# Memory of the RWKV chain becomes ten slots for experts' matrices during the attention, and their loads are issued between its blocks

## Chip, core and metric

The kernel runs on one core of one Trainium2 chip. The metric is the device time of one execution in microseconds (us); lower is better.

## What is computed

One layer of a hybrid encoder on 512 tokens of width 1024, all in float32:

```python
h = rmsnorm(x, norm1_g)
p = h @ w_in                                  # 5504 columns
p_rwkv, q, k, v, gate_logits = split(p)
y_a = rwkv7_bidirectional(p_rwkv, ...) @ w_o_rwkv
y_b = neighbourhood_attention_2d(q, k, v, ...) @ w_o_na
g_a, g_b = split(sigmoid(gate_logits + b_gate))
x = x + (g_a * y_a + g_b * y_b) @ w_out
x = x + hierarchical_moe(rmsnorm(x, norm2_g), ...)   # 32 experts: gate, up, down
```

The last part routes each token to two of 32 experts. An expert is silu(h @ w_gate) * (h @ w_up), times w_down.

## The kernel before

**Stages.** norm1 makes hT, the normalized and transposed input, as a high and a low part. The projection by w_in goes in 43 tiles of 128 columns (proj, L301). Each needs a load of its raw weights on SyncE's queue (w_raw, wraw, 512 KB, two buffers), a high part on ScalarE (ACT, w_hi, L185), a low part (w_lo, L188) on VectorE (DVE), or on GpSimd (POOL) from tile 15 on, and 24 matmuls of 128x512 on TensorE (PE). Tiles 0 to 14 feed the RWKV recurrence; 15 to 42 are the `others` (L759): q, k and v of the attention, then the gates. A gate's result is evacuated from its PSUM bank by ACT (oth) and spilled to DRAM (d_oth). The last nine tiles, 34 to 42, are called b to j here. Matmuls of the `others` have low priority and fill the gaps of the chain and of the attention. The recurrence's second half, `chain(1)`, ends in chain_out, which stores ya (d_ya). The attention (na_attention, L825) goes over two groups of heads and four blocks of columns each, and stores yb (d_yb).

**After the attention.** out_gated (L916) loads ya and yb again (ya_f, yb_f), splits them in high and low parts, multiplies by w_o_rwkv and w_o_na (in_wo) and by the gates (ga, gb), which are fetched from d_oth. out_rows (L977) multiplies by w_out, adds x, transposes and starts the router. Then moe (L1319) works through 16 pairs of experts, 64 rows each: six matrices of 1 MB for a pair (two with gate and up, one down, for each of two experts), 96 in all. It gathers rows xe, transposes them, computes G (gate and up), sg and Yd (down), and adds the result to the output by a scatter. tasks (L1159), called in the second pair, computes a table on VectorE and stores it with SyncE (tab, tabi).

**Slots.** The 96 matrices go through NSLOT = 21 slots (tiles ws0 to ws20) in the order of USE; matrix i takes the slot of matrix i - 21. load_upto(n) (L1242) issues loads until n are out. The slots come in three pools: NS1 = 8 opened after the attention, NS2 = 6 after out_gated, the other 7 after the route. out_gated issues five loads, spread over its eight steps; out_rows issues up to 14 in all; moe issues the rest, after each pair up to 6(p + 1) + 4 + NSLOT.

**What sets the order.** A scheduler orders each engine's instructions by priority and by the order in which the code emits them. Each engine's queue is then fixed: an instruction that waits holds up all behind it. SyncE (SP) issues all loads and stores but the gathers and scatters. Memory is laid out by pools on a left and a right side, and a tile that lies where another has lain waits for that one's last use. The chain's pools are ch (T, 64 KB of each partition; R, 32 KB; O) and cw. Tiles rp (constants, oth) lie left of them.

Of the kernel before, what the change touches and what calls it, by code (L numbers as in the profile page):

```python
# [28 lines left out]
WARM = 12  # L29
NX = 3  # L30
NY = 2
NSLOT = 21
NS1, NS2 = 8, 6
NL1, NL2 = 5, 7
LAG = 2
NT2 = 6
EM05 = float(np.exp(-0.5))
# [141 lines left out]
class K:  # L179
# [645 lines left out]
    def na_attention(self):  # L825
        self.yb = [self.dram.tile([P, 2, 4, P], F32, name="d_yb%d" % i) for i in range(2)]
        for h4 in range(2):
            self.na_inputs(h4)
            for b in range(4):
                self.na_block(h4, b)  # L830
                if 4 * h4 + b < OTH[3]:
                    self.others(1)
        self.others(28, ("x", "mm"))

    def na_block(self, h4, b):
# [80 lines left out]
    def out_gated(self, opz, opw):  # L916

        nc = self.nc
        yaT, ybT = [[opz.tile([P, 4, T], F32R, name="y%s_%s" % (c, n)) for n in ("hi", "lo")] for c in "ab"]

        def part_a(yt):
            t = self.fetch(self.ya[yt], opz.tile([P, T], F32, name="ya_f", tag="ga", bufs=3))
            self.split([y[:, yt] for y in yaT], t)

        def part_b(h4, b, n):
            t = opz.tile([P, 2, n, P], F32, name="yb_f", tag="ga", bufs=3)
            nc.sync.dma_start(t, self.yb[h4][:, :, b:b + n])
            self.split([y[:, 2 * h4:2 * h4 + 2, b * P:(b + n) * P].rearrange("p a (n c) -> p a n c", n=n) for y in ybT], t)

        part_a(0)  # L930
        part_a(1)
        part_b(0, 0, 2)
        part_b(0, 2, 2)
        part_a(2)
        part_a(3)
        part_b(1, 0, 2)
        part_b(1, 2, 1)
        part_b(1, 3, 1)
        self.zT = zT = [[opw.tile([P, 4, T], F32R, name="z%d%s" % (i, n)) for n in ("hi", "lo")] for i in range(2)]
        nat = lambda a: a.rearrange("p (b r c) -> p r b c", b=4, r=8)  # L940
        acc = []

        def open_m(m):
            w = self.wload(m, "wo")
            acc.append((w, [self.bank("mm", [P, T], 4) for c in range(2)]))

        def add(m, c, ks):
            (hi, lo), ps = acc[m]
            y = (yaT, ybT)[c]
            for k in ks:  # L950
                l = [t[:, 4 * c + k] for t in (hi, lo)]
                self.mm3(ps[c], l, [nat(t[:, k]) if c else t[:, k] for t in y], k == 0, k == 3)


        for m in range(2):
            open_m(m)
            for c in range(2):
                add(m, c, range(2))
        for m in range(8):
            if m >= 2:  # L960
                open_m(m)
            for c in (1, 0):
                add(m, c, range(2 if m < 2 else 0, 4))
            pa, pb = acc[m][1]
            ga = self.fetch(self.gate[m], opz.tile([P, T], F32, name="ga", tag="ga", bufs=3))
            gb = self.fetch(self.gate[8 + m], opz.tile([P, T], F32, name="gb", tag="ga", bufs=3))
            self.stt(ga, ga, 1.0, pa, OP.add, OP.mult)
            self.stt(gb, gb, 1.0, pb, OP.add, OP.mult)
            self.tt(ga, ga, gb, OP.add)
            z = [t[:, m % 4] for t in zT[m // 4]]  # L970
            self.act(z[0], ga, AF.Copy, scale=0.5)
            self.stt(z[1], ga, 0.5, z[0].bitcast(F32), OP.mult, OP.subtract)
            if m == 1:
                self.route_setup()
            self.load_upto(NL1 * (m + 1) // 8)

    def out_rows(self):  # L977

        nc, op, zT = self.nc, self.op, self.zT
        x1 = []  # L980
        for tt in range(4):
            x1.append(op.tile([P, D], F32, name="x1_%d" % tt))
            nc.sync.dma_start(x1[-1], self.A["x"][tt * P:(tt + 1) * P])
        rl = self.bank("lg", [P, 4, 36], 1)
        ss = op.tile([P, 2, 4], F32, name="r_ss")

        def post(n, tt, ps):

            x = x1[tt][:, n * T:(n + 1) * T]
            self.tt(x, ps, x, OP.add)  # L990
            sl = slice(tt * P, (tt + 1) * P), slice(n * T, (n + 1) * T)
            nc.sync.dma_start(self.A["out"][sl], x)
            self.act(ps, x, AF.Square, scale=1.0 / 32, accum_out=ss[:, n, tt:tt + 1])
            if n + tt == 0:

                self.act(op.tile([P, 1], F32, name="r_tab"), ss[:, 0, 0:1], AF.Sqrt)
            pt = self.bank("mm", [P, 4, P], 4) if n == 1 and tt >= 2 else self.bank("tp", [P, 4, P], 2)
            for k in range(4):
                self.tr(pt[:, k], x[:, k * P:(k + 1) * P])
            xT = op.tile([P, 4, P], F32, name="x1T", tag="x1T", bufs=2)  # L1000
            if n == 1 and tt == 3:
                nc.vector.tensor_copy(xT[:, 0:2], pt[:, 0:2])
                self.act(xT[:, 2:4], pt[:, 2:4])
            elif tt % 2 == 1:
                self.act(xT, pt)
            else:
                nc.vector.tensor_copy(xT, pt)
            for k in range(4):
                self.mm(rl[:, tt], xT[:, k], self.wr[:, 4 * n + k], start=(n + tt + k == 0), stop=(n == 1 and tt + k == 6),
                        skip_group_check=True)  # L1010
            xg = op.tile([P, T], F32, name="r_xg", tag="r_xg", bufs=2)
            self.tt(xg, x, self.g2[:, sl[1]], eng=nc.gpsimd)
            nc.sync.dma_start(self.h2[sl], xg)

        for n in range(2):
            ps = [self.bank("mm", [P, T], 4) for tt in range(4)]
            w = {}
            for m2 in range(4):
                with self.low(-LOW):
                    hi, lo = [w_.rearrange("p (a k) b -> p a (k b)", a=2) for w_ in self.wload(4 * n + m2, "w_out")]  # L1020
                for i in range(2):
                    w[2 * m2 + i] = hi[:, i], lo[:, i]

                ms = [2 * m2, 2 * m2 + 1] if n == 0 or m2 < 2 else range(4, 8) if m2 == 3 else []
                steps = [(m, tt) for m in ms for tt in range(4)]
                for m, tt in sorted(steps, key=lambda u: u[::-1]) if len(ms) == 4 else steps:
                    sl = slice(tt * P, (tt + 1) * P)
                    self.mm3(ps[tt], tuple(t[:, m % 4, sl] for t in zT[m // 4]), w[m], m == 0, m == 7)
                    if m == 7 and tt >= LAG:
                        post(n, tt - LAG, ps[tt - LAG])  # L1030
                self.load_upto(min(NS1 + NS2, NL1 + (NS1 + NS2 - NL1) * (4 * n + m2 + 1) // NL2))
            for tt in range(4 - LAG, 4):
                post(n, tt, ps[tt])
        st = self.st
        self.stt(st, ss[:, 0], 1e-6, ss[:, 1], OP.add, OP.add)
        self.act(st, st, AF.Sqrt)
        nc.vector.reciprocal(st, st)
        lg = op.tile([P, 4, 36], F32, name="r_lg")
        self.tt(lg, rl, st[:, :, None].to_broadcast([P, 4, 36]))
        self.tt(lg, lg, self.br[:, None].to_broadcast([P, 4, 36]), OP.add)  # L1040
        self.route(lg)
# [324 lines left out]
def build(tc, A):  # L1366
    with ExitStack() as ctx:
        k = K(tc, A, ctx)
# [5 lines left out]
        with ExitStack() as c2:  # L1374
            k.hpool = c2.enter_context(tc.tile_pool(name="hp", bufs=1, side="right"))
            with tc.tile_pool(name="n1", bufs=1) as n1:
                k.norm1(n1)
            k.rp = c2.enter_context(tc.tile_pool(name="rp", bufs=1))
            k.ch = c2.enter_context(tc.tile_pool(name="ch", bufs=1))
            k.cw = c2.enter_context(tc.tile_pool(name="cw", bufs=1))  # L1380
            with tc.tile_pool(name="tmp", bufs=1, side="right") as k.tmp:
                k.rwkv()
            with tc.tile_pool(name="na", bufs=1, side="right", reuse_waits="tile") as k.na:
                k.na_setup()
                k.chain(1)
                k.chain_out(1)
                k.na_attention()
        k.psum_next()
        k.rt = ctx.enter_context(tc.tile_pool(name="rt", bufs=1, reuse_waits="tile"))
        k.wslot, k.slot, k.loaded = [], [], 0  # L1390
        k.slots_open(ctx.enter_context(tc.tile_pool(name="w1", bufs=1, reuse_waits="tile")), NS1)
        cr, cwo = ExitStack(), ExitStack()
        opw = cwo.enter_context(tc.tile_pool(name="opw", bufs=1, side="right", reuse_waits="tile"))
        k.op = cr.enter_context(tc.tile_pool(name="op", bufs=1, side="right", reuse_waits="tile"))
# [35 lines left out]
```

## Time and profile before

| | us |
|---|---|
| median of 3 runs | 939.39 |
| lowest, highest run | 938.81, 946.36 |
| profiled execution | 942.74 |
| its span | 940.6 |

PE is busy 87% of the span, VectorE 46%, ACT 33%, POOL 19%. The profile reads so: a row of a timeline is start, length, engine, line, operation, output<-inputs, count, and in brackets the idle time before it and what ended it. PE is TensorE, PEld its weight loads, SPq the issues of SyncE. In a table of windows a row is the window, its length, the busy time (and instructions) of PE, PEld, DVE, ACT and POOL, the granted clock of TensorE as a share of 2.4 GHz, the mean busy share of the DMA engines, and GB/s. Lines are those of the kernel before; up to the removed lines, the same code stands one line higher after the change.

### The profile page before, as it was taken

The page shows a single profiled execution, that of the slowest core. Times are in us where ns is not written, and L with a number is a line of the kernel's source. Part 1 is how long each engine was busy: PE and PEld are TensorE (multiplying, and loading weights), DVE is VectorE, ACT ScalarE, POOL GpSimd, SP SyncE. Part 2 cuts the span into 40 slices and gives each one's busy share as a digit, 9 for nine tenths or more (in the row PEclk, how much of TensorE's full clock was granted, in tenths as well). Part 3 has the DMA queues.
Part 4 walks back from the last instruction along what each step waited for, and adds up shares of the span by engine and source line. Part 5 has one row for each costly group of instructions (what it writes and reads, how often), then busy time and mean ns, then how long its engine had stood idle before and what let it go on. Part 6 is the DMA issues. An engine that isn't in the chain of part 4 may idle for free. (4 is left out here: it accounts for less than half of the span.)

```text
span 940.6 us, 17281 instructions
## 1 busy us (share of the span) xinstructions
PE 817.8 (87%) x7192; PEld 526.8 (56%) x7192; DVE 430.7 (46%) x870; ACT 309.0 (33%) x667; POOL 177.6 (19%) x154
## 2 busy tenths in 40 slices
PE   8999887889988987799998999999489999788884
PEld 7676655556666655566676678878333333233321
DVE  5698883565689588224446405732412111011000
ACT  6444521223433553035747623232211121011101
POOL 2611121120003132132312330012302112111001
PEclk9999995999998999699999999999689999999998
DMA  6321121121122322322314648889877999999982
GB/s 223 101 64 40 35 101 36 57 69 57 36 68 71 121 68 67 118 80 63 103 51 129 205 138 311 306 314 368 339 314 273 389 395 401 395 403 401 403 337 42
DMA packets 49774, 176.17 MB, mean 187 GB/s; under 512 B 7584, under 2 KB 14368, under 8 KB 37664
## 3 DMA queue, kind: packets, MB, share of 16 engines
q1 hardware_dynamic: 45088, 166.66, 48.1%
q0 software_dynamic: 4608, 8.40, 3.7%
q8 instruction: 57, 0.93, 0.4%
q14 instruction: 21, 0.17, 0.1%
HBM read 159.30 MB, written 24.12 MB: 195 GB/s over the span
## 5 line engine op out<-in xcount | busy, mean ns | idle before, releaser
L200 PE MATMUL G<-ws,xT 128*64 128x512 f32 x512 | 131.4, 603 | 11.0 <-DMA ws<-in_wgu 9.3
L200 PE MATMUL mm<-hT_hi,w_lo 128*128 128x512 f32 x264 | 114.2, 433 | 7.9 <-ACT oth L185 6.8
L188 POOL TENSOR_TENSOR w_lo<-w_raw,w_hi 128x1024 fp32r<-128x1024 f32 x29 | 70.6, 2435 | 241.6 <-ACT w_hi L185 241.6
L200 PE MATMUL mm<-hT_hi,w_hi 128*128 128x512 f32 x264 | 111.9, 424 | 0.0
L200 PE MATMUL mm<-hT_lo,w_hi 128*128 128x512 f32 x264 | 111.8, 423 | 0.0
L200 PEld LDWEIGHTS G<-ws,xT 128*64 128x64 f32 x512 | 42.4, 138 | 87.3 <-issue 64.6
L200 PE MATMUL Yd<-ws,hT 128*64 128x512 f32 x256 | 68.2, 606 | 8.2 <-ACT y L185 8.2
L185 ACT ACTIVATE w_hi<-w_raw 128x1024 fp32r<-128x1024 f32 x59 | 62.3, 1055 | 29.5 <-PE mm L200 29.0
L200 PEld LDWEIGHTS mm<-hT_hi,w_lo 128*128 128x128 f32 x264 | 52.1, 197 | 26.3 <-issue 15.4
L188 DVE TENSOR_TENSOR w_lo<-w_raw,w_hi 128x1024 fp32r<-128x1024 f32 x30 | 37.1, 1237 | 50.7 <-ACT w_hi L185 50.7
L200 PEld LDWEIGHTS mm<-hT_lo,w_hi 128*128 128x128 f32 x264 | 52.0, 197 | 12.8 <-issue 2.2
L200 PEld LDWEIGHTS mm<-hT_hi,w_hi 128*128 128x128 f32 x264 | 52.0, 197 | 11.5 <-issue 1.7
L188 DVE TENSOR_TENSOR sg<-sg,G 128x256 f32<-128x256 f32 x16 | 6.7, 420 | 109.4 <-ACT sg L185 109.4
L1362 POOL DMA_INDIRECT out<-y,idx x16 | 25.3, 1580 | 135.5 <-DVE y L195 106.9
L185 ACT ACTIVATE sg<-G,wts 128x256 f32<-128x256 f32 x16 | 7.6, 473 | 117.7 <-PE G L200 117.7
L648 DVE COPY R<-c 32x128 f32<-32x128 f32 x64 | 18.7, 293 | 54.0 <-ACT R L185 53.3
L200 PE MATMUL c<-R,T 128*32 128x64 f32 (+1 forms) x992 | 36.3, 231 | 7.9 <-DVE nrs_i L191 2.2
L195 DVE TENSOR_SCALAR y<-Yd,wts 128x512 f32<-128x512 f32 (+1 forms) x16 | 11.8, 734 | 68.2 <-PE Yd L200 61.6
L200 PEld LDWEIGHTS Yd<-ws,hT 128*64 128x64 f32 x256 | 17.4, 136 | 44.4 <-ACT y L185 21.2
L200 PE MATMUL tp<-T,KB 64*64 64x128 f32 x512 | 35.0, 281 | 7.3 <-ACT T L185 7.1
L200 PEld LDWEIGHTS c<-R,T 128*32 128x32 f32 (+1 forms) x992 | 26.2, 125 | 26.5 <-issue 14.0
L185 ACT ACTIVATE T<-tp 64x256 f32<-64x256 f32 x64 | 23.9, 377 | 45.0 <-DVE T L188 44.1
(312 smaller groups left out, 1465.5 us busy)
## 6 DMA issues: line engine op xcount, KB each, us to landing
ws<-in_wgu SPq DMA_DIRECT2D x64, 1024.0 KB, 19.6
ws<-in_wd SPq DMA_DIRECT2D x30, 1024.0 KB, 21.0
w_raw<-in_w_in SPq DMA_DIRECT2D x43, 512.0 KB, 3.7
d_oth<-oth SPq DMA_DIRECT2D x16, 256.0 KB
w_raw<-in_wo SPq DMA_DIRECT2D x8, 512.0 KB, 3.8
w_raw<-in_w_out SPq DMA_DIRECT2D x8, 512.0 KB, 5.7
x_in<-in_x SPq DMA_DIRECT2D x4, 512.0 KB, 6.8
ga<-d_oth SPq DMA_DIRECT2D x8, 256.0 KB
```

The source lines that it names most:

```text
L185: self.nc.scalar.activation(out, in_, func, **kw)
L188: (eng or self.nc.vector).tensor_tensor(out, a, b, op=op)
L195: self.nc.vector.tensor_scalar(out, a, s1, None, op0=op0)
L200: return self.nc.tensor.matmul(out, l, r, start=start, stop=stop, **kw)
L648: self.nc.vector.tensor_copy(R[u, :, blk, p2], ps[u, 2:4])
L1362: self.nc.gpsimd.indirect_dma_start(out=self.A["out"], out_offset=bass.IndirectOffsetOnAxis(ap=idx, axis=0), in_=y, in_offset=None, bounds ...
```

## The change

The pools ch and cw get a context of their own (c3) and are closed after the chain's last use, before na_attention. In their place lie the pool rt and the ten slots of w1 (NS1 = 10 instead of 8). na_attention issues the loads of these ten, one or two after each block. out_gated issues none. out_rows issues one a step, to 15 in all (NS2 = 5); the third pool still has 7 slots, so NSLOT is 22. The pool rp moves to the right side, and na is opened in c2. The tiles of out_gated (opz) lie higher by 16 KB of each partition, over the attention's nam, bias, qT and kT instead of the chain's T and R. VectorE's eight small operations of rwkv_consts, which need rp, no longer wait for norm1's memory, and move ahead of the scales of norm1's tiles 1 to 3. On POOL, the copies into T move ahead of the second projection's w_lo.

```diff
--- before.py
+++ after.py
@@ -29,9 +29,8 @@
 WARM = 12
 NX = 3
 NY = 2
-NSLOT = 21
-NS1, NS2 = 8, 6
-NL1, NL2 = 5, 7
+NSLOT = 22
+NS1, NS2 = 10, 5
 LAG = 2
 NT2 = 6
 EM05 = float(np.exp(-0.5))
@@ -830,6 +829,7 @@
                 self.na_block(h4, b)
                 if 4 * h4 + b < OTH[3]:
                     self.others(1)
+                self.load_upto(NS1 * (4 * h4 + b + 1) // 8)
         self.others(28, ("x", "mm"))
 
     def na_block(self, h4, b):
@@ -972,7 +972,6 @@
             self.stt(z[1], ga, 0.5, z[0].bitcast(F32), OP.mult, OP.subtract)
             if m == 1:
                 self.route_setup()
-            self.load_upto(NL1 * (m + 1) // 8)
 
     def out_rows(self):
 
@@ -1028,7 +1027,7 @@
                     self.mm3(ps[tt], tuple(t[:, m % 4, sl] for t in zT[m // 4]), w[m], m == 0, m == 7)
                     if m == 7 and tt >= LAG:
                         post(n, tt - LAG, ps[tt - LAG])
-                self.load_upto(min(NS1 + NS2, NL1 + (NS1 + NS2 - NL1) * (4 * n + m2 + 1) // NL2))
+                self.load_upto(NS1 + min(NS2, 4 * n + m2 + 1))
             for tt in range(4 - LAG, 4):
                 post(n, tt, ps[tt])
         st = self.st
@@ -1375,20 +1374,21 @@
             k.hpool = c2.enter_context(tc.tile_pool(name="hp", bufs=1, side="right"))
             with tc.tile_pool(name="n1", bufs=1) as n1:
                 k.norm1(n1)
-            k.rp = c2.enter_context(tc.tile_pool(name="rp", bufs=1))
-            k.ch = c2.enter_context(tc.tile_pool(name="ch", bufs=1))
-            k.cw = c2.enter_context(tc.tile_pool(name="cw", bufs=1))
-            with tc.tile_pool(name="tmp", bufs=1, side="right") as k.tmp:
-                k.rwkv()
-            with tc.tile_pool(name="na", bufs=1, side="right", reuse_waits="tile") as k.na:
+            k.rp = c2.enter_context(tc.tile_pool(name="rp", bufs=1, side="right"))
+            with ExitStack() as c3:
+                k.ch = c3.enter_context(tc.tile_pool(name="ch", bufs=1))
+                k.cw = c3.enter_context(tc.tile_pool(name="cw", bufs=1))
+                with tc.tile_pool(name="tmp", bufs=1, side="right") as k.tmp:
+                    k.rwkv()
+                k.na = c2.enter_context(tc.tile_pool(name="na", bufs=1, side="right", reuse_waits="tile"))
                 k.na_setup()
                 k.chain(1)
                 k.chain_out(1)
-                k.na_attention()
+            k.rt = ctx.enter_context(tc.tile_pool(name="rt", bufs=1, reuse_waits="tile"))
+            k.wslot, k.slot, k.loaded = [], [], 0
+            k.slots_open(ctx.enter_context(tc.tile_pool(name="w1", bufs=1, reuse_waits="tile")), NS1)
+            k.na_attention()
         k.psum_next()
-        k.rt = ctx.enter_context(tc.tile_pool(name="rt", bufs=1, reuse_waits="tile"))
-        k.wslot, k.slot, k.loaded = [], [], 0
-        k.slots_open(ctx.enter_context(tc.tile_pool(name="w1", bufs=1, reuse_waits="tile")), NS1)
         cr, cwo = ExitStack(), ExitStack()
         opw = cwo.enter_context(tc.tile_pool(name="opw", bufs=1, side="right", reuse_waits="tile"))
         k.op = cr.enter_context(tc.tile_pool(name="op", bufs=1, side="right", reuse_waits="tile"))
```

ACT, before, from the evacuation of projection d to that of h. Here oth_5215, 5325, 5425, 5516 and 5618 are the evacuations of d, e, f, g and h; w_hi_5396, 5487, 5589 and 5624 the splits of the weights of f, g, h and i.

```order
L185 ACTIVATE oth_5215<-mm_5190,hb_229 128x512
L185 ACTIVATE w_hi_5396<-w_raw_5394 128x1024
L185 ACTIVATE yb_5531<-tp_5580 64x256
L185 ACTIVATE ya_hi_5724<-ya_f_5748 128x512
L185 ACTIVATE yb_hi_5726<-yb_f_5752 128x2x256
L185 ACTIVATE yb_hi_5726<-yb_f_5756 128x2x128
L185 ACTIVATE oth_5325<-mm_5300,hb_229 128x512
L185 ACTIVATE w_hi_5487<-w_raw_5485 128x1024
L185 ACTIVATE yb_hi_5726<-yb_f_5760 128x2x128
L185 ACTIVATE oth_5425<-mm_5400,hb_229 128x512
L185 ACTIVATE w_hi_5589<-w_raw_5587 128x1024
L185 ACTIVATE oth_5516<-mm_5491,hb_229 128x512
L185 ACTIVATE w_hi_5624<-w_raw_5622 128x1024
L185 ACTIVATE oth_5618<-mm_5593,hb_229 128x512
```

After, from the evacuation of e on. Here oth_5348, 5449, 5541 and 5644 are e, f, g and h; w_hi_5420, 5512, 5615, 5652 and 5687 the splits of f, g, h, i and j.

```order
L184 ACTIVATE oth_5348<-mm_5323,hb_229 128x512
L184 ACTIVATE w_hi_5420<-w_raw_5418 128x1024
L184 ACTIVATE w_hi_5512<-w_raw_5510 128x1024
L184 ACTIVATE oth_5449<-mm_5424,hb_229 128x512
L184 ACTIVATE w_hi_5615<-w_raw_5613 128x1024
L184 ACTIVATE oth_5541<-mm_5516,hb_229 128x512
L184 ACTIVATE oth_5644<-mm_5619,hb_229 128x512
L184 ACTIVATE w_hi_5652<-w_raw_5650 128x1024
L184 ACTIVATE w_hi_5687<-w_raw_5685 128x1024
```

The split of f has moved from behind the evacuation of d to behind that of e, that of i from behind g to behind h; the splits of ya and yb are no longer between them.

SP, before, around the load of f's weights (w_raw_5394) to that of g's (w_raw_5485).

```order
L288 DMA w_raw_5394<-in_w_in 128x1024
L904 DMA d_yb1_4815<-yb_5340 256x1x128
L560 DMA bvr_4798<-d_bv2_3178 128x512
L560 DMA gr_4801<-d_g2_1076 128x512
L560 DMA bvr_4806<-d_bv3_4012 128x512
L560 DMA gr_4809<-d_g3_1082 128x512
L556 DMA d_oth20_5115<-oth_5113 128x512
L556 DMA d_ya2_4804<-y_4768 128x512
L288 DMA w_raw_5485<-in_w_in 128x1024
```

SP, after, from the slot ws4 on, with f's weights (w_raw_5418); oth_5236 and oth_5348 are d and e.

```order
L1260 DMA ws4_4826<-in_wd 128x2048
L555 DMA d_ya2_4804<-y_4768 128x512
L555 DMA d_ya3_4812<-y_4769 128x512
L904 DMA d_yb1_4833<-yb_5261 256x1x128
L555 DMA d_oth21_5238<-oth_5236 128x512
L1260 DMA ws5_4827<-in_wd 128x2048
L904 DMA d_yb1_4833<-yb_5364 256x1x128
L287 DMA w_raw_5418<-in_w_in 128x1024
L1260 DMA ws6_4828<-in_wgu 128x2048
```

The load of f's weights stood ahead of a store of yb and of the fetches for the chain's output; now it stands behind the evacuation of d and behind the load of ws5.

SP in moe, before, around the store of the table. Loads into ws0 to ws6 here are second uses of these slots, so 26 loads are issued ahead of it (21 first uses, and 0 to 3 and 6).

```order
L1261 DMA ws20_6650<-in_wgu 128x2048
L1261 DMA ws0_5707<-in_wgu 128x2048
L1261 DMA ws1_5708<-in_wd 128x2048
L1261 DMA ws2_5709<-in_wd 128x2048
L1261 DMA ws3_5710<-in_wgu 128x2048
L1261 DMA ws6_5713<-in_wgu 128x2048
L1186 DMA tab_6777<-t_tab_6767 128x2
L1187 DMA tabi_6778<-t_ti_6774 128x2
L1261 DMA ws4_5711<-in_wgu 128x2048
```

The same place after, where slots 0 to 3, 6 and 7 are used again ahead of the table, 28 loads in all.

```order
L1260 DMA ws0_4822<-in_wd 128x2048
L1260 DMA ws1_4823<-in_wd 128x2048
L1260 DMA ws2_4824<-in_wgu 128x2048
L1260 DMA ws3_4825<-in_wgu 128x2048
L1260 DMA ws6_4828<-in_wd 128x2048
L1260 DMA ws7_4829<-in_wd 128x2048
L1185 DMA tab_6779<-t_tab_6769 128x2
L1186 DMA tabi_6780<-t_ti_6776 128x2
L1260 DMA ws4_4826<-in_wgu 128x2048
L1260 DMA ws5_4827<-in_wgu 128x2048
```

Two more loads stand ahead of the table's store than before: one more first use and one more second use.

## Rows read from the trace of the kernel before

**Rows 1.** Windows of 20 us (columns as said under the profile above)
```profile
540.00:560.00 20.00, 18.51 (x80) 15.05 (x81) 0.00 (x0) 6.18 (x8) 7.18 (x3) 1.00 0.43 138
720.00:740.00 20.00, 20.00 (x89) 6.89 (x86) 3.07 (x5) 2.83 (x5) 5.08 (x4) 1.00 1.02 402
840.00:860.00 20.00, 15.89 (x62) 5.09 (x59) 2.08 (x4) 2.61 (x5) 2.63 (x2) 1.00 1.01 397
```

**Rows 2.** PE's timeline in the experts
```profile
740.81 0.51 PE L1300 MATMUL tp<-cst,sg 128*128 128x128 f32 x2
...
753.93 0.50 PE L1300 MATMUL tp<-cst,sg 128*128 128x128 f32 x2
...
860.26 0.50 PE L1300 MATMUL tp<-cst,sg 128*128 128x128 f32 x2 [1.02 <-DVE sg L188]
...
871.70 3.65 PE L200 MATMUL G<-ws,xT 128*64 128x512 f32 x14 [0.81 <-DMA ws<-in_wgu]
876.37 0.51 PE L1300 MATMUL tp<-cst,sg 128*128 128x128 f32 x2 [1.02 <-DVE sg L188]
```

**Rows 3.** The page's DMA issues: KB each, median us to landing
```profile
ws<-in_wgu SPq DMA_DIRECT2D x64, 1024.0 KB, 19.6
...
w_raw<-in_w_in SPq DMA_DIRECT2D x43, 512.0 KB, 3.7
...
w_raw<-in_w_out SPq DMA_DIRECT2D x8, 512.0 KB, 5.7
```

**Rows 4.** SP's timeline around the table's store, route to experts
```profile
667.51 24.65 SPq L1261 DMA_DIRECT2D ws<-in_wgu  x4
...
708.82 0.34 SPq L1186 DMA_DIRECT2D tab<-t_tab  x1
```

**Rows 5.** A window of 4 us behind the table's store
```profile
708.00:712.00 4.00, 3.23 (x18) 1.03 (x16) 1.43 (x9) 0.69 (x1) 0.00 (x0) 1.00 0.23 53
```

**Rows 6.** Timeline of ACT, POOL and PE around projections e to i
```profile
533.12 0.69 ACT L185 ACTIVATE oth<-mm,hb 128x512 f32<-128x512 f32 x1 [2.32 <-PE mm L200]
533.70 1.05 ACT L185 ACTIVATE w_hi<-w_raw 128x1024 fp32r<-128x1024 f32 x1
...
553.03 0.69 ACT L185 ACTIVATE oth<-mm,hb 128x512 f32<-128x512 f32 x1 [5.01 <-issue]
...
534.83 2.39 POOL L188 TENSOR_TENSOR w_lo<-w_raw,w_hi 128x1024 fp32r<-128x1024 f32 x1 [4.33 <-ACT w_hi L185]
...
533.95 0.47 PE L200 MATMUL mm<-hT_hi,w_lo 128*128 128x512 f32 x1 [0.87 <-ACT oth L185]
...
552.78 0.39 PE L200 MATMUL x<-hT_hi,w_lo 128*128 128x512 f32 x1
```

**Rows 7.** PE's timeline at two long waits, and the windows behind them
```profile
105.27 1.36 PE L200 MATMUL tp<-T,KB 64*64 64x128 f32 x16 [2.76 <-ACT T L185]
...
301.37 1.12 PE L203 MATMUL c<-cst,yc 128*128 128x128 f32 x4 [4.08 <-POOL yc L188]
...
105.90:109.30 3.40, 3.40 (x29) 2.37 (x23) 2.72 (x6) 1.14 (x3) 0.00 (x0) 0.51 0.02 5
301.30:307.30 6.00, 5.93 (x18) 4.98 (x19) 4.08 (x6) 3.88 (x15) 2.79 (x2) 0.50 0.34 108
```

**Rows 8.** POOL's and PE's timeline at the start
```profile
14.82 0.95 POOL L354 MEMSET O<- 128x1024 f32 x1 [14.36 <-PE Y L200]
...
18.94 2.40 POOL L188 TENSOR_TENSOR w_lo<-w_raw,w_hi 128x1024 fp32r<-128x1024 f32 x1 [2.81 <-ACT w_hi L185]
21.41 3.81 POOL L360 COPY T<-id 64x2048 f32<-64x2048 f32 x2
...
21.39 0.50 PE L200 MATMUL mm<-hT_hi,w_lo 128*128 128x512 f32 x1 [0.29 <-POOL w_lo L188]
...
28.54 0.50 PE L200 MATMUL x<-hT_hi,w_lo 128*128 128x512 f32 x1 [1.41 <-DVE w_lo L188]
```

**Rows 9.** PE's timeline, out_gated's and out_rows' border
```profile
613.69 0.50 PE L200 MATMUL mm<-w_lo,z0hi 128*128 128x512 f32 x1 [1.13 <-DVE gb L191]
```

## Prediction

> **What bounds the kernel now.** I read the windows of 20 us first. In the last projections TensorE (PE) is busy 18.51 of 20 us at full clock, and the DMA engines carry 0.43 of what they can [rows 1]. In the experts' first half (720 to 740) PE is busy for all 20 us, and the DMA engines too (1.02); at 840 to 860 PE has only 15.89 us of work, with the DMA at 1.01 and 397 GB/s. So three stages have three limits: projections go by PE, the first pairs of experts by PE, the last pairs by the loads. PE's timeline says the same: a pair of experts takes 13.12 us where nothing waits (740.81 to 753.93) and 16.11 us later (860.26 to 876.37), with a wait that a load of ws ends [rows 2]. A matrix is 1,024 KB [rows 3], 1.0486 MB; at 400 GB/s (between the 397 and 402 of rows 1) it takes 2.62 us, and six of them with their gathers and scatters make the 16.11.
>
> It follows that the end is worth 2.62 us for each matrix by which the stream of loads stands further ahead there, and that the attention and the projections pay for any microsecond by which PE waits. The change touches both.
>
> **The change, part by part.**
>
> *The slots: a gain at the end.* How far ahead loads can be is capped by slots, not by when the first loads were issued: 22 instead of 21. Ten of them are filled during the attention, where the DMA has room, but by the route's end before has 14 of its slots loaded too, and the change 15. So the ten early loads are worth one load, 2.62 us, not ten. A second one may come from the stall on SP: its queue reaches the table's store, which runs at 708.82 only when VectorE has written it, and behind it the loads stand still [rows 4]; the DMA share is 0.23 in the four microseconds from 708 [rows 5]. By the order, 26 loads are issued ahead of that store before and 28 after. This is worth two loads at most, 5.24 us. I take 4.4: nearer to two, since the stall is on the path of the loads and both loads go out ahead of it; the ends are 2.6 and 5.3.
>
> *The split of weights: a cost in the attention's tail.* Each of the last projections (I call them d to j, as front does) needs three steps before PE can start: the load, w_hi on ScalarE (ACT), w_lo on GpSimd (POOL). Before, ACT splits the weights of f right behind the evacuation of d, and those of g at 533.70, behind that of e [rows 6]: two projections ahead. So PE waits 0.87 us at 533.95, for the evacuation of its bank alone, and starts i at 552.78 with no wait. After, the order of ACT puts the split of f behind the evacuation of e, and the split of i behind that of h, because the loads of f's and i's raw weights stand later in SP's queue, behind matrices' loads. From the start of an evacuation to the end of the POOL split that follows it takes 533.12 to 534.83 + 2.39 = 537.22, thus 4.10 us [rows 6]. PE would start f at about 537.25 instead of 533.95: +3.3. Projection i started 0.25 us ahead of h's evacuation (552.78 against 553.03); it would start 4.13 behind it: +4.4. The other projections keep one to two steps of lead: while PE runs one (f, g and h take 533.95 to 552.78, 6.3 us each, rows 6), the next one's 4.1 us fit. Sum +7.7. Bounds: 0, if the loads and splits come earlier than the order suggests, and +12, if a third projection (h) falls behind too.
>
> *TensorE's clock after the two gaps.* After PE waited 2.76 us at 105.27 and 4.08 us at 301.37, the granted clock was 0.51 and 0.50 in the windows that follow, 3.4 and 6 us long: the lower of its two levels, 1.2 GHz instead of 2.4 [rows 7]. Matmuls take twice as long there, so half of the window is lost: 1.7 and 3.0 us, 2.35 in the mean. Gaps of 0.87 us brought no fall: the window from 540 has 1.00 [rows 1]. Gaps of 4 us are at the size of the second; I take 2.15 a gap, +4.3 for two. Bounds 0 and +6.
>
> *The start.* rwkv's small tiles lie elsewhere, and this moves instructions of the first 30 us. Before, VectorE has eight small operations (rwkv_consts) between the norm's last scale and the third projection's w_lo, for which PE waits 1.41 us at 28.54 [rows 8]; after, they stand among the norm's first scales: −1.4. But on POOL the two copies into T, 3.81 us, stand ahead of the second projection's w_lo now. Before, that ran from 18.94 to 21.34. Before, O's memset ends at 14.82 + 0.95 = 15.77; the copies behind it would end at 19.6 and w_lo at 22.0. PE, which started at 21.39, 0.05 behind w_lo, would start 0.7 later: +0.7. Net −0.7, with ends −1.7 and +1.5.
>
> *out_gated.* Before, five loads of matrices run there, and a gate's load comes late: PE waits 1.13 us for gb at 613.69 [rows 9]. After, no matrix is loaded in it: −1.0 (0 to −1.1). Against that, ya and yb are fetched and split only behind h's evacuation, since their memory is that of the attention's tiles now. Nine fetches and splits lie beside i and j, some 13 us of PE, so I cost them at nothing; if that cover is gone, a fetch of about 3.7 us [rows 3] stands open.
>
> Sum: −0.7 + 7.7 + 4.3 − 1.0 − 4.4 = +5.9. The profiled execution took 942.74 (span 940.6), so the changed kernel would take 948.6 by it. That execution is 3.35 above the median of the runs, 939.39; against the median I say 945.3.
>
> Two rules of the Trainium skill bear on this. "Perfetto Trace Analysis", section "Optimization Strategy", says that where the most contended engine changes over time, "performance may be improved by interleaving those regimes": ten loads at 2.62 us moved from the last stage to the attention would be −26. The trace shows both regimes, but here slots cap the lead; it is rival C. "DMA: Bandwidth & Descriptors", section "Queues, rings and completion order", has each DMA engine take descriptors of one ring in order, so weights issued behind a matrix wait for it; the row that agrees is the w_out weights' landing time among matrices, 5.7 against 3.7 us [rows 3]. It is rival B.
>
> **The rivals.**
>
> *A: the order on ACT is not what PE meets.* Evacuations and splits are queued as written, but if f's and i's splits cost PE no more than a short wait, or if the clock doesn't fall, what stays is the gain: −0.7 − 1.0 − 4.4 = −6.1 without any gap, 933.3; with the gaps but full clock +1.6, 941.0. For it: gaps of 0.9 do no harm. Against: the queue order is fixed at build, and 4.1 us have no cover.
>
> *B: slower. The weights wait behind matrices on the DMA.* Place: projections f to j, whose loads stand on SP behind ws5 to ws9. In the crowded stage a weight's load lands 2.0 us later (5.7 less 3.7, rows 3). Where such a lateness adds to each of five projections, the price is 5 times 2.0, +10, on top of +5.9: 955.3. It decides from the point where a load lands later than a projection's 6.3 us less the 4.1 of its split, 2.2 us behind the previous evacuation. For it: w_raw's 3.7 exceed that where it is issued at the evacuation. Against: most are issued a projection ahead.
>
> *C: the stages interleave fully.* −26, and with the tail's cost (+7.7 + 4.3) and the two other gains (−0.7 − 1.0) −15.9: 923.5. Against: 22 slots against 21, and the DMA at 1.01 from 720 on, in either kernel.
>
> *D: the gain at the end doesn't come,* because the stall on the table only moves: +5.9 + 4.4 = +10.3, 949.7. For it: four loads issued from 667.51 on take 24.65 us to get out, while the table's store that stands behind them is not yet due, so slots that come free late can set the pace and not SP's order [rows 4].
>
> **How the numbers follow.** Forecast 0.45, A 0.29 (its two forms about even), D 0.18, B 0.06, C 0.02. One per cent is 9.4 us, about what a measurement of this kernel can tell from no change: faster means below 930.0, slower above 948.8. The forecast's own spread from its bounds is some 5 us, so about a fifth of it is slower; with over half of D and most of B, slower holds 0.23; faster has C and a little of A's form without gaps, 0.05; the same 0.72. The range from 932.5 to 952 leaves out C, most of B, and the ends of A and D, under 0.2 together.
>
> **What would show it.** Right: PE idle about 4 us ahead of two of the last projections, released by POOL w_lo, and a granted clock near 0.5 after each; no wait for gb in out_gated; the last pairs of experts still at 16 us each, the stretch from the gather to the end 3 to 5 us shorter; DMA share above 0.5 in the attention's windows. Wrong: PE back to back from d to j (A), waits of w_hi on its load there (B), a pair of 13 us near the end (C), or the end of the experts as long as before (D).

## Result and profile after

The changed kernel takes 951.5 us (median of 12 runs, 945.3 to 955.7), the kernel before 940.0 (12 runs beside them, 937.3 to 946.4). The ratio is 1.0115, with an interval of 1.0087 to 1.0143: slower by about 11 us, where +5.9 was forecast. The profiled execution took 955.7, the longest of the twelve, with a span of 953.6, 13.0 more than that of before. What follows breaks up these 13.0, not the median's difference. The time between marks that both timelines have:

| stage, by PE's timeline | before | after | difference |
|---|---|---|---|
| start to the recurrence's last run of Y matmuls | 489.77 | 490.25 | +0.48 |
| from there to projection f | 44.18 | 50.73 | +6.55 |
| f to out_gated's first matmul | 30.70 | 39.78 | +9.08 |
| out_gated to the first transpose of gathered rows | 120.19 | 122.62 | +2.43 |
| from there to the sg transpose of the last pair | 234.82 | 229.31 | −5.51 |
| from there to the end | 20.94 | 20.91 | −0.03 |

PE's timeline before, at the marks that are not shown above and at two places that the text comes back to (58.46 and 503.02):

```profile
58.46 1.10 PE L200 MATMUL tp<-kd,cst 128*128 128x512 f32 x2 [1.69 <-DVE kd L191]
...
489.77 1.76 PE L200 MATMUL Y<-R,T 128*32 128x64 f32 x109 [0.71 <-issue]
...
503.02 0.44 PE L203 MATMUL tp<-cst,s 128*128 128x128 f32 x2 [0.86 <-ACT s L185]
...
564.65 0.50 PE L200 MATMUL mm<-ya_lo,w_hi 128*128 128x512 f32 x1 [0.83 <-ACT oth L185]
...
684.84 1.94 PE L1271 MATMUL tp<-cst,xe 128*128 128x128 f32 x8 [7.86 <-DMA xe<-h,idx]
...
919.66 0.51 PE L1300 MATMUL tp<-cst,sg 128*128 128x128 f32 x2 [1.01 <-DVE sg L188]
```

PE's timeline after (columns as in [rows 2]):

```profile
22.31 0.50 PE L199 MATMUL mm<-hT_hi,w_lo 128*128 128x512 f32 x1 [0.97 <-POOL w_lo L187]
...
57.71 1.69 PE L199 MATMUL tp<-kd,cst 128*128 128x512 f32 x2 [1.69 <-DVE kd L190]
...
490.25 1.76 PE L199 MATMUL Y<-R,T 128*32 128x64 f32 x108 [1.00 <-issue]
...
504.59 0.66 PE L199 MATMUL x<-kT,qT 64*128 64x128 f32 x4 [1.55 <-DVE s L187]
...
540.98 0.79 PE L199 MATMUL mm<-hT_hi,w_lo 128*128 128x512 f32 x1 [4.14 <-POOL w_lo L187]
...
566.52 0.69 PE L199 MATMUL x<-hT_hi,w_lo 128*128 128x512 f32 x1 [4.19 <-POOL w_lo L187]
...
580.76 0.50 PE L199 MATMUL mm<-ya_lo,w_hi 128*128 128x512 f32 x1 [1.49 <-ACT oth L184]
...
630.75 0.50 PE L199 MATMUL mm<-w_lo,z0hi 128*128 128x512 f32 x1 [1.82 <-DVE gb L190]
...
703.38 1.94 PE L1270 MATMUL tp<-cst,xe 128*128 128x128 f32 x8 [7.78 <-DMA xe<-h,idx]
...
873.30 0.51 PE L1299 MATMUL tp<-cst,sg 128*128 128x128 f32 x2 [1.02 <-DVE sg L187]
...
889.40 0.51 PE L1299 MATMUL tp<-cst,sg 128*128 128x128 f32 x2 [1.02 <-DVE sg L187]
...
932.69 0.51 PE L1299 MATMUL tp<-cst,sg 128*128 128x128 f32 x2 [1.01 <-DVE sg L187]
```

The two waits ahead of f (540.98) and i (566.52) are the ones foreseen, where [rows 6] had 0.87 and none. A pair near the end still takes 16.1 us (873.30 to 889.40), as in [rows 2]. The chain ahead of f, on ACT and on POOL:

```profile
536.88 0.69 ACT L184 ACTIVATE oth<-mm,hb 128x512 f32<-128x512 f32 x1 [1.21 <-PE mm L199]
537.47 1.05 ACT L184 ACTIVATE w_hi<-w_raw 128x1024 fp32r<-128x1024 f32 x1
```

```profile
538.59 2.34 POOL L187 TENSOR_TENSOR w_lo<-w_raw,w_hi 128x1024 fp32r<-128x1024 f32 x1 [15.66 <-ACT w_hi L184]
```

Evacuation of e, split of f, low part: 536.88 to 540.93, 4.05 us. Windows after, in the columns of [rows 1], at four places where the granted clock fell, and one near the start:

```profile
58.00:90.00 32.00, 30.92 (x310) 22.54 (x310) 28.13 (x46) 12.23 (x25) 3.22 (x2) 0.95 0.24 75
...
507.00:512.00 5.00, 5.00 (x17) 3.69 (x17) 1.80 (x4) 2.98 (x8) 1.82 (x3) 0.50 0.10 40
541.00:546.00 5.00, 5.00 (x12) 3.94 (x13) 0.00 (x0) 1.06 (x1) 1.90 (x1) 0.50 1.01 381
566.50:570.00 3.50, 3.48 (x9) 2.72 (x10) 3.04 (x3) 1.69 (x3) 2.30 (x1) 0.52 0.76 224
630.00:634.00 4.00, 3.25 (x9) 2.62 (x10) 2.07 (x3) 0.63 (x1) 0.00 (x0) 0.69 0.84 350
634.00:638.00 4.00, 4.00 (x17) 3.20 (x17) 1.23 (x1) 1.06 (x1) 0.00 (x0) 0.88 0.00 0
```

At 0.50 a window of 5 us loses 2.5 us. These rows account for nearly all of three stages. To f: 3.27 longer wait (4.14 less 0.87), 0.7 longer wait at 504.59 (1.55, where before had 0.86), 2.5 clock: 6.5 of 6.55. To out_gated: 4.19, then 2.5 and 1.7 clock, and 0.66 at 580.76 (1.49, before 0.83): 9.05 of 9.08. To the gathered rows: 0.69 longer wait for gb (1.82 against 1.13 in [rows 9]), and 1.7 clock (0.31 and 0.12 of the two windows of 4 us from 630): 2.4 of 2.43.

SyncE around the table's store, which answers to [rows 4]:

```profile
709.60 0.80 SPq L1260 DMA_DIRECT2D ws<-in_wd  x2
713.04 0.80 SPq L1260 DMA_DIRECT2D ws<-in_wgu  x2
718.02 0.80 SPq L1260 DMA_DIRECT2D ws<-in_wd  x2
726.60 0.34 SPq L1185 DMA_DIRECT2D tab<-t_tab  x1
...
728.99 13.93 SPq L1260 DMA_DIRECT2D ws<-in_wgu  x6
```

Loads 28 and 29 (wd, at 718.02) go out 8.6 us before the store; before, they stood behind it.

### The profile page after: what moved, and what is told of

Its sections match the earlier page's. It is cut to its first block, busy times and chain, and to the rows that moved or that the text cites. A ratio compares the mean times of both kernels' runs of the same rounds, so it can differ in the third digit from the quotient of the medians.

```text
span 953.6 us, 17274 instructions
## 1 busy us (share of the span) xinstructions
PE 825.1 (87%) x7192; PEld 535.8 (56%) x7192; DVE 424.8 (45%) x870; ACT 309.6 (32%) x667; POOL 178.7 (19%) x154
```

## Experiments

All are compared with the kernel before, run on the same chip in the same rounds; its medians there are 938.9 to 940.3. Three theories of the loss: **O**, the queue order in the attention's tail; **T**, the traffic of 1 MB loads beside it; **L**, the layout, by which ya and yb are fetched late. Two stages of each profile tell most, by the marks of the table above:

| kernel | median us | ratio, interval | recurrence's end to out_gated | experts' stage |
|---|---|---|---|---|
| before | | 1 | 74.88 | 234.82 |
| after | 951.5 | 1.0115, 1.0087 to 1.0143 | 90.51 | 229.31 |
| e1_slots22 | 940.1 | 1.0014, 0.9988 to 1.0041 | 74.83 | 234.15 |
| e2_layout_only | 937.6 | 0.9998, 0.9968 to 1.0028 | 75.45 | 228.88 |
| e3_eight | 938.4 | 0.9988, 0.9962 to 1.0013 | 75.55 | 228.87 |
| e4_after_attention | 943.6 | 1.0045, 1.0017 to 1.0072 | 75.84 | 228.12 |
| e7_first5 | 955.6 | 1.0202, 1.0161 to 1.0243 | 94.87 | 229.14 |
| e8_table_gpsimd | 939.6 | 1.0000, 0.9974 to 1.0026 | 74.84 | 234.36 |
| e11_ring4 | 935.0 | 0.9937, 0.9912 to 0.9962 | 78.19 | 228.81 |
| e13_fill | 942.6 | 1.0024, 0.9990 to 1.0058 | 85.60 | 230.37 |
| e14_order22 | 938.8 (one run) | | 74.96 | 233.72 |
| e15_order21_table | 937.9 | 0.9970, 0.9950 to 0.9989 | 74.87 | 231.70 |
| e17_order22_table | 937.1 | 0.9955, 0.9937 to 0.9974 | 74.84 | 229.38 |
| e18_order_table_ring4 | 932.8 | 0.9905, 0.9885 to 0.9926 | 74.87 | 229.52 |

### Where the tail's loss comes from

**e2_layout_only**, the changed kernel with the loads back where they were:

```diff
-                self.load_upto(NS1 * (4 * h4 + b + 1) // 8)
...
                 self.route_setup()
+            self.load_upto(5 * (m + 1) // 8)
...
-                self.load_upto(NS1 + min(NS2, 4 * n + m2 + 1))
+                self.load_upto(min(NS1 + NS2, 5 + (NS1 + NS2 - 5) * (4 * n + m2 + 1) // 7))
```

> The changed kernel with its memory, slots and pools, but the loads issued where they were before (five over out_gated's steps, the rest in out_rows); the scheduler then puts five of them into the tail by itself, behind the weights of the projections. Theory O: no PE wait of 4 us before projections f and i, 934 to 938. Rival L (layout: ya's and yb's tiles lie over the attention's, so they are fetched and split late): a wait at out_gated's start of 1 us or more remains, 945 or above. Rival T (traffic: 1 MB loads beside the tail's weights and small transfers cost by their number): half of the loss, about 944.

937.6, and the tail takes 75.45 us: both waits are gone. L falls for the tail, but in out_gated there is a wait for gb of 2.13 us, so the stage behind it takes 122.60 us, as in the changed kernel.

**e3_eight**, the changed kernel with another split of the 22 slots:

```diff
-NS1, NS2 = 10, 5
+NS1, NS2 = 8, 7
```

> The changed kernel with eight instead of ten slots (and loads) in the attention and seven instead of five behind it. By the order, f's and i's splits stand again two projections ahead, while the eight loads are issued between the blocks as in the changed kernel. Theory O: no PE wait of 4 us in the tail; 936 to 940. Rival T (traffic): eight tenths of the loss, 948 or above.

938.4; PE's timeline ahead of f:

```profile
503.80 0.66 PE L199 MATMUL x<-kT,qT 64*128 64x128 f32 x4 [1.55 <-DVE s L187]
...
534.29 0.47 PE L199 MATMUL mm<-hT_hi,w_lo 128*128 128x512 f32 x1 [0.87 <-ACT oth L184]
```

Eight loads go out between the same blocks, and PE waits only for the evacuation. T falls: eight of the ten loads are there, and the tail takes 0.67 us more than before, not 15.6. By the code, f's weights are written behind the sixth block: with ten slots six loads are written ahead of them (10·5//8), with eight five. One load less ahead was enough to put f's and i's splits back two projections ahead.

**e4_after_attention**, all ten loads written behind the last projections:

```diff
-                self.load_upto(NS1 * (4 * h4 + b + 1) // 8)
         self.others(28, ("x", "mm"))
+        self.load_upto(NS1)
```

> The changed kernel with all ten loads written behind the last projections instead of between the attention's blocks. All ten still go out in the tail, but each behind a projection's weights. Theory O: no PE wait of 4 us before f and i, 934 to 939. Rival T: as many loads beside the tail as in the changed kernel, so no better than 948. Rival L: ya and yb are fetched as late as in the changed kernel, so 943 or above, with the time lost at out_gated's start.

943.6: above what O said, though the tail has no wait of 4 us (75.84). The loss that the profile shows is in out_gated, whose stage takes 126.27 us, 6.1 more than before (the profiled execution, 937.1, is the shortest of the ten, so it does not show all of the median's loss):

```profile
559.44 0.50 PE L199 MATMUL mm<-ya_lo,w_hi 128*128 128x512 f32 x1 [1.22 <-ACT oth L184]
...
574.49 0.50 PE L199 MATMUL mm<-yb_lo,w_hi 128*128 128x512 f32 x1 [2.88 <-ACT w_hi L184]
```

Behind the wait of 2.88 us the granted clock was 0.50 for 3.4 us (576.2 to 579.6). The fetches of ya and yb stand behind all ten loads, and out_gated's weights behind the first of those fetches. That is so in the changed kernel too, but there the first fetch goes out 17.3 us ahead of out_gated's first matmul (563.50 to 580.76), here 10.9 (548.57 to 559.44). So L has its price too, where the fetches come this late.

**e7_first5**, all ten loads written ahead of f's weights:

```diff
-                self.load_upto(NS1 * (4 * h4 + b + 1) // 8)
+                if 4 * h4 + b < 5:
+                    self.load_upto(2 * (4 * h4 + b + 1))
```

> The changed kernel with the ten loads written behind the first five blocks, two each: all ten stand in SyncE's queue ahead of f's weights, but i's weights ahead of g's evacuation. Theory O: one wait of 4 us or more, before f (longer than 4.1 if the weights land behind four matrices: up to 10), none before i; 940 to 948. Rival T: 948 or above with the time spread over the tail, no single wait of 4 us. Rival L: as the changed kernel at out_gated's start.

955.6, above O's 948, and within T's "948 or above", but not spread over the tail as T had it: the time stands in single long waits. There is one ahead of f and none of 4 us ahead of i, as O expected, but another, longer one stands ahead of f's:

```profile
530.48 1.12 PE L202 MATMUL tp<-cst,s 128*128 128x128 f32 x4 [7.14 <-ACT yb L184]
...
543.02 0.80 PE L199 MATMUL mm<-hT_hi,w_lo 128*128 128x512 f32 x1 [3.97 <-POOL w_lo L187]
```

On ACT, the step that PE waits for:

```profile
530.05 0.78 ACT L184 ACTIVATE yb<-tp 64x256 f32<-64x256 f32 x2 [5.99 <-DMA d_yb<-yb]
```

ACT can't write a third yb into its two buffers until the first is stored. That store stands on SyncE behind loads, and behind the store of a projection's result, for which the queue waits 5.8 us. It is the same cause, a queue in order, at a second place. Behind the 7.14 the granted clock stays at 0.50 until 546: in the tail PE is busy 73.67 us where before it is 67.89, so the clock took some 5.8 us of the 20 that the tail is longer.

**e13_fill**, the changed kernel with added matmuls in the two waits:

```diff
         with self.low(by):
+            if m in (38, 41):
+                fill = self.bank("c0", [P, T], 1)
+                for _ in range(20):
+                    self.mm(fill, self.last[:, 0], hh[:, 0])
+            self.last = hi
```

> The changed kernel with 20 matmuls added ahead of projection f and 20 ahead of i, into a bank that nobody reads (added work, the output is the same); by the order 16 of each fall into the wait for the split, some 3.6 us of its 4.1. Theory K (the granted clock falls because PE waits 4 us there, and costs 2.3 us behind f and 1.8 behind i): the clock stays at 1.0 in f and i and the time is about 4 us less than the changed kernel's, 947.5. Rival: the clock's fall has another cause, or f and i aren't on the path: 951.5 or more.

942.6. PE's timeline at f, and the window behind it:

```profile
534.26 3.79 PE L199 MATMUL c<-hT_hi,w_hi 128*128 128x512 f32 x16
538.61 0.50 PE L199 MATMUL mm<-hT_hi,w_lo 128*128 128x512 f32 x1 [0.56 <-POOL w_lo L187]
```

```profile
538.00:544.00 6.00, 5.44 (x25) 4.42 (x24) 0.00 (x0) 1.06 (x1) 2.47 (x2) 1.00 0.97 342
```

The projection starts hardly earlier (50.38 us behind the recurrence's last Y matmuls, 50.73 in the changed kernel), but the clock stays at 1.00. From f to out_gated it takes 35.22 us (538.61 to 573.83) instead of 39.78: 4.56 less, of which 4.2 are the clock of the two windows above. The median gained 9.0, so half of it lies elsewhere: in this profile PE has no wait for gb of 0.75 us or more, and that stage takes 118.55. That part isn't the filling's doing as far as these runs show.

### Where the gain at the end comes from

**e1_slots22**, the kernel before with one slot more:

```diff
-NSLOT = 21
-NS1, NS2 = 8, 6
+NSLOT = 22
+NS1, NS2 = 8, 7
```

> The kernel before with one slot more (22: 8, 7 and 7) and nothing else: no pool moved, the first loads after the attention as before. Theory O (order: the loss comes from where the loads stand in SyncE's queue in the attention's tail, and the slots gain about 5 us at the end): some 935, 5 below before. Theory N (the extra slot gains nothing, what the changed kernel won at the end is only its earlier loads): as before, 940.

No gain: the experts' stage takes 234.15. The slot alone is worth 0.7 at most.

**e8_table_gpsimd**, the kernel before with the table's stores on another queue:

```diff
-        nc.sync.dma_start(self.tab, tab)
-        nc.sync.dma_start(self.tabi, ti)
+        nc.gpsimd.dma_start(self.tab, tab)
+        nc.gpsimd.dma_start(self.tabi, ti)
```

> The kernel before (21 slots, nothing moved) with the two stores of the experts' table issued by GpSimd instead of SyncE, so that no load stands behind them. Theory S (the experts' stage was shortened because 28 instead of 26 loads are out before the table's store blocks SyncE): the stage from the first transpose of gathered rows to the last pair is 4 to 6 us shorter than before, 934. Rival: it is the 22nd slot together with the loads' lead, and the queue's stall costs nothing: as before, 939.

No gain either, against theory S. SyncE's timeline tells why:

```profile
692.63 16.34 SPq L1261 DMA_DIRECT2D ws<-in_wgu  x4
709.03 1.18 SPq L1261 DMA_DIRECT2D ws<-in_wd  x2
```

Without the store, the queue stands at the next loads: the last two of the four in the first row go to slots 4 and 5, which hold pair 0's down matrices until about 709. Two reasons stop the queue at nearly the same time. So theory W, which the next three kernels test: what counts is how many loads are out by then.

**e14_order22** writes the loads for the slots 6 and 7, which come free earlier, ahead of those for 4 and 5 (on top of e1); **e17_order22_table** has e8's edit as well; **e15_order21_table** is the same with 21 slots (the numbers 25 to 28):

```diff
-            p, j, e2 = USE[self.loaded]
             i = self.loaded
-            self.slot.append(i if i < NSLOT else self.slot[i - NSLOT])
+            if 26 <= i < 30:
+                i += 2 if i < 28 else -2
+            p, j, e2 = USE[i]
...
-        k.wslot, k.slot, k.loaded = [], [], 0
+        k.wslot, k.slot, k.loaded = [], [i % NSLOT for i in range(96)], 0
```

> e1_slots22 (the kernel before with 22 slots) with the loads 28 and 29, whose slots 6 and 7 come free early, written ahead of 26 and 27, which wait for pair 0's down matrices in slots 4 and 5. SyncE still meets the table's store ahead of them. Theory W (what counts is how many loads are out before SyncE stands still at about 708, for the table or for slots 4 and 5, whichever comes first in its queue: 26 before, 28 in the changed kernel; 2.6 us for each): still 26 out, so the experts' stage from the first transpose to the last pair is as in e1, 234. Rival (the order of these loads alone): 229.

> The kernel before with its 21 slots, the loads 27 and 28 (slots 6 and 7) written ahead of 25 and 26 (slots 4 and 5), and the table's two stores issued by GpSimd: 27 loads out before the queue stands still. Theory W: one load more than before, so the experts' stage takes 232.2 instead of 234.8 and the whole some 936. Rival (a 22nd slot is needed): 234.8, 939.

> e14_order22 with the table's two stores issued by GpSimd: 22 slots, 28 loads out before the queue stands still, nothing changed ahead of the experts. Theory W: the experts' stage takes 229 to 230 as in the changed kernel, the whole some 934. Rival (the gain needs the early loads or the moved pools): 234, 939.

233.72, 231.70 and 229.38 us for the stage: 26, 27 and 28 loads out before the stop. Each load is worth 2.2 to 2.7 us (from e1's 234.15 or e14's 233.72 with 26 loads to e17's with 28, and from e8's 234.36 with 26 to e15's with 27), near the 2.62 of the estimate, and 21 or 22 slots matter only by that count. The whole gained somewhat less than expected: 937.9 for 936 with 27 loads, 937.1 for 934 with 28. SyncE in e15_order21_table:

```profile
697.75 0.39 SPq L1262 DMA_DIRECT2D ws<-in_wd  x1
708.31 0.80 SPq L1262 DMA_DIRECT2D ws<-in_wgu  x2
```

and in e17_order22_table:

```profile
701.17 0.80 SPq L1262 DMA_DIRECT2D ws<-in_wd  x2
712.14 13.93 SPq L1262 DMA_DIRECT2D ws<-in_wgu  x6
```

One load more than before goes out ahead of the stop in the first, two in the second. Neither needs a load during the attention.

### out_gated

**e11_ring4**, e2_layout_only with four buffers in the ring (only the argument that changes is shown, it stands in four places):

```diff
-tag="ga", bufs=3
+tag="ga", bufs=4
```

> e2_layout_only with four instead of three buffers for the gates and ya, yb fetches in out_gated. Theory R (the gate's fetch waits for a buffer of its ring, lands 4 to 5 us later and PE waits for it, behind which the clock falls): no wait for gb of over 0.5 us, out_gated's start to the first transpose of gathered rows some 120 us instead of 122.6; 935. Rival: the fetch waits for its place in SyncE's queue, so the wait stays, 937.6.

935.0, and 117.81 us for the stage instead of 122.60. In the changed kernel VectorE waits for the gate's fetch, and PE behind it:

```profile
630.01 0.69 DVE L190 SCALAR_TENSOR_TENSOR gb<-gb,mm 128x512 f32<-128x512 f32 x1 [1.89 <-DMA gb<-d_oth]
```

The same wait of PE in e2_layout_only, with loads in this stage, and in e3_eight, without:

```profile
612.41 0.50 PE L199 MATMUL mm<-w_lo,z0hi 128*128 128x512 f32 x1 [2.13 <-DVE gb L190]
```

```profile
613.96 0.50 PE L199 MATMUL mm<-w_lo,z0hi 128*128 128x512 f32 x1 [1.08 <-DVE gb L190]
```

In e11_ring4 the last two gates come nearly or fully in time:

```profile
603.26 0.69 DVE L190 SCALAR_TENSOR_TENSOR gb<-gb,mm 128x512 f32<-128x512 f32 x1 [0.61 <-DMA gb<-d_oth]
...
608.11 0.68 DVE L190 SCALAR_TENSOR_TENSOR gb<-gb,mm 128x512 f32<-128x512 f32 x1
```

So the wait is the ring's: a fetch can't be issued until a buffer comes free, and lands 4.0 us later (median of the eight of gb in the changed kernel, 5.0 at most). With four buffers it lands no faster (4.2), but the last one is issued 36.9 us behind out_gated's first matmul, where e2_layout_only has 43.8.

**e18_order_table_ring4** is e17_order22_table with this edit.

> e17_order22_table with four instead of three buffers in out_gated's ring of fetches: the version put together from what the runs showed. Theory W and theory R together: 5 us off in the experts and 1 to 2 in out_gated (before had waits for gates of 1.1 us at most, and no fall of the clock behind them), 932 to 934. If the ring gains only where the pools were moved: as e17.

932.8, 0.9905 of before (0.9885 to 0.9926): faster than both kernels, with no load in the attention and no pool moved. Its stage from out_gated to the gathered rows takes 118.53, 1.7 less than before and less than the 119.04 to 120.43 of all six kernels with three buffers and no pool moved.

## Why the prediction was wrong

- *The sign and the tail's waits: right.* "+3.3" and "+4.4" for f and i were 3.27 and 4.19, and the clock fell behind both, so rival A fell. The cause is the order of the queues, not the traffic as such: with eight of the ten loads in the attention both waits are gone (e3_eight).
- *The clock behind the two gaps: right in size*, 4.2 against 4.3, and e13_fill shows that it is PE's idleness in the wait that costs it.
- *The first step that failed: "out_gated … After, no matrix is loaded in it: −1.0 (0 to −1.1)".* In this profile it was +2.4: without any load, the wait grew from 1.13 to 1.82, and the clock fell behind it. The loads were not why the gate came late. With matrices loaded there, PE waits 2.13 us for gb (e2_layout_only), 1.30 (e8_table_gpsimd) or less than 0.75 (e1_slots22); without any, 1.94 (e4_after_attention), 1.32 (e7_first5), 1.08 (e3_eight) or less than 0.3 (e13_fill). What decides is the ring of three buffers (e11_ring4, which loads five matrices there and has no such wait). I took the nearest neighbour in the queue for the cause, without asking when the fetch had been issued. Of the 7.1 us by which this profile's 13.0 exceeds the +5.9, these 3.4 are nearly half. But the size is in part this execution's: e3_eight, e7_first5 and e13_fill, with the same code in this stage, take 120.61, 119.76 and 118.55 us for it, and before took 120.19.
- *The second step that failed, and the larger one over all runs: "TensorE's clock after the two gaps … +4.3 for two" counts no fall of the clock elsewhere.* In the new layout, PE waits 1.55 us at 504.59 for VectorE; why VectorE comes later there is open. In three of seven profiles with that wait (the changed kernel, e11_ring4, e13_fill) the granted clock fell to 0.50 behind it; it cost 2.5 in the changed kernel's, and with 0.7 of longer wait these 3.2 are the other half of the 7.1. In the others, e3_eight's among them, it stayed at 1.00. Each run's span and mean granted clock tell what such falls come to over all executions. The mean clock is 0.944 in the changed kernel (median of 12 runs), 0.948 in e3_eight (10 runs), which has neither gap, and 0.952 in the kernel before (31 runs beside e3_eight's). What the mean lacks to 1, times the span, is 53, 49 and 45 us. By this estimate, which is an upper bound because it also counts stretches in which PE has nothing to do, the clock took some 8 us of the loss where 4.3 were foreseen: about 4 behind the two gaps, and about 4 that e3_eight lost too. The rest of the span is 888 us in e3_eight and 893 before, 5 less, where the forecast without the two gaps and their clock has −6.1. So by this estimate most of the median's miss (11.6 for 5.9) is clock outside the two gaps. Profiles show it behind the wait at 504.59 and behind two waits for gb (1.82 and 2.13); how it is shared between these and other places is open.
- *out_gated's start, costed at nothing:* 0.66 longer wait. The cover of two projections nearly held.
- *The start: right until 58 us.* The second projection began 0.92 later (22.31, forecast 0.7), the third's wait of 1.41 went, and at 57.71 the kernel was 0.75 ahead (58.46 before), as the −0.7 said. It was lost again from 58 to 90, where the clock was 0.95 in this execution and 1.00 before.
- *The end: −5.5 for −4.4, for a reason half right.* Two more loads ahead of the stop were worth nearly two loads, but the stop is not the table's store alone, as the text had it. e8_table_gpsimd took that away and gained nothing; slots 4 and 5 stop the queue just as long. Rival D fell, as the gain came, though its argument, that slots which come free late can set the pace, is what e8_table_gpsimd shows. C fell too: the ten early loads as such gained nothing, and e17_order22_table has the whole gain without them.
- *Rival B* (weights late on the DMA by 2.0 us each in five projections) fell by e3_eight.

## What to carry to other kernels

A load with slack that was put into a queue in order competed here by its place, not by its bandwidth: ask which small, urgent issues now stand behind it, and write background loads behind the weights that the next steps need. The depth of the prefetch was here the number of transfers out before the queue first stopped; when two reasons stop it at the same time, taking away one shows nothing, so list all that would stop it next before calling a stall the cause. Where an engine waits for a fetch, look first at when its buffer came free. One profile shows the falls of the clock in one execution; the mean granted clock of every run, times its span, shows what they come to in all.

## What was not expected of the hardware

The same wait of PE, 1.55 or 1.56 us in the same place, was followed by a clock of 0.50 in three profiles and of 1.00 in four, so here the length of the wait alone did not tell whether the clock falls. Behind waits of 4.14 and 4.19 us it fell in the changed kernel both times, and with 16 matmuls in each of them it fell neither time (e13_fill). Behind waits for gb of 1.82 and 2.13 us it fell (the changed kernel, e2_layout_only), behind one of 1.94 it did not (e4_after_attention).
